# Transposes of a feed-forward's first chunk, and the affine step of two norms, placed differently in a fused three-block kernel

## The chip, the cores and the metric

The kernel runs on one core of a Trainium2 chip. The metric is the device time of one execution in microseconds (us); lower is better. The core has five engines with a queue of instructions each, and each works its queue in order: TensorE (PE, the matrix products), VectorE (DVE), ScalarE (ACT), GpSimd (POOL) and SyncE (SP, which here only starts DMAs).

## What is computed

The input x has 256 tokens of 1024 features, all in float32. A first block runs once: modulation of x by a vector c, an attention and convolution mixer, a layer norm, a gated feed-forward, a second layer norm. Two more layers follow: gated linear attention, feed-forward and a gate; then differential attention, feed-forward and a gate. Of the reference, what the change touches:

```python
def layer_norm(x, g, b):
    mu = mean(x); var = mean(square(x - mu))
    return (x - mu) * rsqrt(var + EPS) * g + b

# first block
x = layer_norm(ALPHA * x + g1 * mix, ln1_g, ln1_b)                 # norm 1
ff = swiglu(modulate(x, sh2, sc2), w_gate, w_up, w_down)           # feed-forward 0
x = layer_norm(ALPHA * x + g2 * ff, ln2_g, ln2_b)                  # norm 2

def swiglu(h, w_gate, w_up, w_down):                               # D_FF = 2816
    return (silu(h @ w_gate) * (h @ w_up)) @ w_down

# end of each of the two layers
h = h + swiglu_2(rms_norm(h), w_in, w_out)                         # feed-forwards 1 and 2
h = h + sigmoid(rms_norm(h) @ ple_w_gate) * (p @ ple_w_proj)
```

## The kernel before

**Products.** The tokens are two tiles of 128 (`t` = 0, 1). Every float32 product is made of three faster ones: an operand is split into a rounded part and a remainder (`xh`, `xl` for activations, `wh`, `wl` for weights), and `mm3` issues `xh*wh` (L159), `xh*wl` (L160) and `xl*wh` (L162). Weights come in granules of 128x1024: SP starts the DMA into `st`, ACT rounds it to `wh` (L150), DVE subtracts to get `wl` (L151). There are 11 buffers for `st` and 5 each for `wh` and `wl`. PSUM has four buffers of 128x512 for products (`mmb`) and four that hold sums for longer (`acb`).

**Order.** The code is a list of steps. A scheduler places each step in the queue of its engine when the program is built, by a cost model of its own, and puts in the waits. It may place a step earlier than the code does, where its operands allow, so what stands in a queue is not the order of the code alone.

**Activations for a product.** A tile of x is transposed by PE in blocks of 128x128 (`blocks_t`, L124) into an `acb`. `put` (L174) then makes `xh` on ACT (L177) and `xl` on DVE (L178). The two norms go through `put_affine` (L193): four ACT instructions per half of a tile (L197, one per block, 128x128) scale and shift the transposed block into `hT`, an SBUF tile with two buffers, and `put` works from there. The halves are `n` = 0 and 1.

**A norm** (`norm_tile`, L773, once for each `t`): DVE adds the product of the feed-forward or the mixer to x; ACT squares with a running sum (L785, `jk`); a few operations on one column give mean and inverse deviation (`mu`, one of them a power on POOL, L787); ACT normalizes each half of x in place (L791), PE transposes it, and `put_affine` follows with weight and offset folded into per-row scale and shift. The residual stream itself needs x times weight plus offset as well: `normed` (L798) multiplies by `g` (L799) and adds `b` (L800), each 128x1024 from a broadcast of the vector over all partitions (`bcast`, a DMA). Norm 1 has it on DVE, given as a fill to chunks 1 and 3 of the feed-forward behind it; norm 2 has it on POOL (`later`). `g2_part` and `g2_row` (L728 to L736) make a vector needed for norm 2 from a product with a column, between the two tiles of norm 1.

**A feed-forward** (`ffn`, L803): 11 chunks of 256 hidden columns. A chunk is four granules of 12 products each, 48 in all, into two `mmb`, one per tile, gate in the left half and up in the right half. The hidden part follows: silu on ACT (L833 in feed-forward 0, L836 in 1 and 2), times up on DVE (L834, L837) into `sg`, four transposes on PE (L124) into a third `mmb`, rounding on ACT (`hh`, L842) and remainder on DVE (`hl`). The second product of chunk c-1 stands between the first product of chunk c and its hidden part. Chunk 0 has nothing of that kind.

**The end** (`fin`, L901): per tile and half, sigmoid on ACT (L904), times a product on DVE (L905), added to x (L906), and a DMA to the output (L1139), 128x512 each.

Of the kernel before, what the change touches and what calls it, by code (L numbers as in the profile page):

```python
# [10 lines left out]
F32 = mybir.dt.float32  # L11
# [3 lines left out]
OP = mybir.AluOpType  # L15
# [67 lines left out]
def body(ctx, tc, d, out, dbg=None):  # L83
# [80 lines left out]
    class XT:  # L164
# [28 lines left out]
        def put_affine(self, t, n, ps, scale, shift, pool, **kw):  # L193
            m = pool.tile([P, 512], F32, name="hT", **kw)
            for i in range(4):
                j = slice(4 * n + i, 4 * n + i + 1)
                A.activation(m[:, i * P:(i + 1) * P], ps[:, i * P:(i + 1) * P], AF.Identity,  # L197
                             bias=shift[:, j], scale=scale[:, j])
            self.put(t, n, m)
# [89 lines left out]
    def block1(adp):  # L289
        with ExitStack() as es:  # L290
# [433 lines left out]
            out_rows(7)  # L724
            l1g = bcast(d["ln1_g"][0], D)
            l1b = bcast(d["ln1_b"][0], D)

            def g2_part(hf):  # L728
# [23 lines left out]
            g2_row(1, *g2[1])  # L752
        with tc.tile_pool(name="f1", bufs=1) as wk:
            acc = ffn(gate_up([(d["w_gate"][0], 0), (d["w_up"][0], 0)]), d["w_down"][0], hx, None, wk,
                      {1: lambda: normed(V, l1g, l1b, 0), 3: lambda: normed(V, l1g, l1b, 1)})
            hx = XT()
# [9 lines left out]
            def later(junk):  # L766
                for t in range(2):
                    normed(G, l2g, l2b, t)
                for t in range(2):
                    rms_of(t, junk, rs[t])  # L770
# [32 lines left out]
    def ffn(gu, wd, xt, rs, wk, fill={}, apart=False):  # L803
# [7 lines left out]

        for c in range(NCH):
            ps = [mm(), mm()]
            for g in range(KB // 2):
                wh, wl = gran(stage(gu(g, c)), (2, 512))
                for t in range(2):
                    for i in range(2):
                        kb = g * 2 + i
                        xh, xl = xt(kb, t)
                        mm3([ps[t]], xh, xl, [wh[:, i]], [wl[:, i]], kb == 0, kb == KB - 1)  # L820
            if c in fill:
                fill[c]()
            if 0 < c < NCH - 1:
                for i in range(2):
                    wh, wl = row_gran(wd, (c - 1) * 2 + i)
                    for t in range(2):
                        both(acc[t], *hid(c - 1, i)(t), wh, wl, c == 1 and i == 0, False)
            tp = mm()
# [14 lines left out]
            V.tensor_sub(hl, tv, hh.bitcast(F32))  # L843
            pend.append((hh, hl))
        late = []
        for c in range(NCH - 2, NCH):
# [50 lines left out]
    def ple_gate(i, xt, rs, pp, wk):  # L897
        acc = accs()
        kproj(d["ple_w_gate_2"][i], INORDER, xt, acc, 4, pool=wk, own=4)

        def fin(t, n):  # L901
            hs = slice(n * 512, n * 512 + 512)
            sg = wk.tile([P, 512], F32, name="sgm", tag="sgm", bufs=2)
            A.activation(sg, acc[t][n], AF.Sigmoid, scale=rs[t])  # L904
            V.tensor_mul(sg, sg, pp[t][:, hs])  # L905
            V.tensor_add(x[t][:, hs], x[t][:, hs], sg)  # L906
        return fin
# [200 lines left out]
    def tail_layer(i, acc, pp, nxt):  # L1108
        with tc.tile_pool(name=f"tl{i}", bufs=1) as wk:
# [25 lines left out]
            for t in range(2):  # L1135
                for n in range(2):
                    hs = slice(n * 512, n * 512 + 512)
                    fin(t, n)
                    Y.dma_start(out[0, t * P:(t + 1) * P, hs], x[t][:, hs])  # L1139

# [195 lines left out]
```

## Time and profile before

| | |
|---|---|
| median of 3 runs | 1066.44 us (1065.1 to 1066.7) |
| profiled execution | 1059.51 us |
| its span, from the first instruction to the last | 1057.7 us |
| granted TensorE clock, mean over the span | 0.991 of full speed |
| PE busy | 1014.9 us, 96% of the span |
| DVE busy | 631.4 us, 60% |
| ACT busy | 560.5 us, 53% |
| POOL busy | 56.3 us, 5% |
| DMA | 57% of the span of 16 engines, 183 GB/s from and to memory |

How to read it: an instruction waits in its queue until its operands are there, and all behind it on that engine wait too. The view of the timeline lists start, duration and, in brackets, the idle time just before and what ended it. The end of a product on PE is modelled, so that its duration overlaps the next one's start; the distance of starts is the time that it takes in a row of products. The chain of waits is followed back from the last instruction to whatever released each step. The rows are shown further down.

### The profile page before, as it was taken

The numbers are of one execution on the slowest core, as the hardware profiler recorded it, in microseconds if no ns is written. First come the engines' busy times: TensorE is split into PE (matmuls) and PEld (weight loads), VectorE is DVE, ScalarE is ACT, GpSimd is POOL, SyncE is SP. The second block draws the span as 40 slices with busy tenths as digits, with TensorE's granted clock in tenths as the row PEclk, the third lists the DMA queues.
The fourth block names the chain that finished last, engine by engine and source line by source line (L and its number), as shares of the span: only waits on it lengthen the run. The fifth ranks groups of instructions, "written<-read, shape, count | busy, mean of one in ns | idle before, by whom it ended". The sixth has DMA issues, their size and how long they took to land.

```text
span 1057.7 us, 13558 instructions
## 1 busy us (share of the span) xinstructions
PE 1014.9 (96%) x4883; PEld 810.6 (77%) x4883; DVE 631.4 (60%) x1021; ACT 560.5 (53%) x910; POOL 56.3 (5%) x47
## 2 busy tenths in 40 slices
PE   6899998999999999999999999999998999999998
PEld 3676675888888778887788888887777778888886
DVE  2378468555556466567554547578786655555654
ACT  2355448444454568465544446566857554444643
POOL 0000100000000130000000000004020100000000
PEclk9999999999999999999999999999999999999999
DMA  9958577866666155255666657535433365666601
GB/s 301 386 200 308 202 276 263 273 195 185 193 196 198 50 175 186 81 166 156 194 190 180 192 187 266 147 127 171 135 120 111 124 187 191 186 190 187 239 1 40
DMA packets 131640, 194.48 MB, mean 184 GB/s; under 512 B 10562, under 2 KB 93390, under 8 KB 131572
## 3 DMA queue, kind: packets, MB, share of 16 engines
q1 hardware_dynamic: 130792, 193.21, 57.0%
q8 instruction: 38, 0.62, 0.2%
q10 hardware_dynamic: 780, 0.40, 0.1%
q14 instruction: 30, 0.25, 0.1%
HBM read 192.53 MB, written 1.05 MB: 183 GB/s over the span
## 4 chain that ended last, share of the span: by engine, by line
PE 79%; DVE 8%; ACT 6%; DMA 2%; issue 2%; POOL 1%; SPq 0%; ACTq 0%; DVEq 0%; POOLq 0%
PE mmb L162 16%; PE mmb L159 16%; PE mmb L160 16%; PE acb L162 7%; PE acb L159 7%; PE acb L160 7%; DVE wl L151 2%; PE mmb L124 2%; ACT wh L150 1%; PE acb L124 1%; POOL rs L272 1%; ACT e L1202 1%; DMA st<-in_w_ada_dram 1%; PE mmb L333 1%; PE acb L333 1%
## 5 line engine op out<-in xcount | busy, mean ns | idle before, releaser
L151 DVE TENSOR_TENSOR wl<-st,wh 128x1024 fp32r<-128x1024 f32 (+4 forms) x292 | 350.9, 1207 | 240.1 <-ACT wh L150 237.2
L150 ACT CAST wh<-st 128x1024 fp32r<-128x1024 f32 (+4 forms) x292 | 300.6, 1038 | 280.6 <-PE mmb L162 143.6
L159 PE MATMUL mmb<-wh,xh 128*128 128x512 f32 (+4 forms) x888 | 353.4, 399 | 6.3 <-ACT xh L386 4.5
L160 PE MATMUL mmb<-wl,xh 128*128 128x512 f32 (+4 forms) x888 | 346.8, 391 | 2.1 <-DVE wl L151 2.1
L162 PE MATMUL mmb<-wh,xl 128*128 128x512 f32 (+4 forms) x888 | 342.8, 391 | 6.0 <-DVE xl L178 4.7
L159 PEld LDWEIGHTS mmb<-wh,xh 128*128 128x128 f32 x888 | 169.1, 191 | 44.7 <-ACT xh L386 6.3
L162 PEld LDWEIGHTS mmb<-wh,xl 128*128 128x128 f32 x888 | 169.1, 190 | 44.5 <-DVE xl L178 6.3
L160 PEld LDWEIGHTS mmb<-wl,xh 128*128 128x128 f32 x888 | 169.3, 191 | 33.3 <-DVE wl L151 2.8
L159 PE MATMUL acb<-wh,hh 128*128 128x512 f32 x216 | 84.0, 389 | 0.0
L160 PE MATMUL acb<-wl,hh 128*128 128x512 f32 x216 | 84.0, 389 | 0.0
L162 PE MATMUL acb<-wh,hl 128*128 128x512 f32 x216 | 66.6, 389 | 0.0
L159 PEld LDWEIGHTS acb<-wh,hh 128*128 128x128 f32 x216 | 40.6, 188 | 8.4
L162 PEld LDWEIGHTS acb<-wh,hl 128*128 128x128 f32 x216 | 40.5, 188 | 8.4
L160 PEld LDWEIGHTS acb<-wl,hh 128*128 128x128 f32 x216 | 40.5, 188 | 8.4
L866 POOL TENSOR_TENSOR rsx<-rsx,mhalf 128x1 f32<-128x1 f32 x12 | 10.2, 851 | 468.2 <-DVE rsx L865 468.2
L272 POOL TENSOR_TENSOR rs<-rs,mhalf 128x8 f32<-128x8 f32 (+1 forms) x14 | 20.0, 1433 | 241.1 <-DVE rs L271 241.1
L836 ACT ACTIVATE sg<-mmb,rsx 128x256 f32<-128x256 f32 x44 | 20.7, 474 | 22.2 <-PE mmb L162 20.4
L151 DVE TENSOR_TENSOR wxl<-st,wxh 128x1024 fp32r<-128x1024 f32 x22 | 26.7, 1219 | 3.1 <-ACT wxh L150 3.1
L837 DVE SCALAR_TENSOR_TENSOR sg<-mmb,rsx,sg 128x256 f32<-128x256 f32 x44 | 20.8, 480 | 11.1 <-ACT sg L836 11.1
L150 ACT CAST wxh<-st 128x1024 fp32r<-128x1024 f32 x22 | 22.7, 1052 | 5.1 <-PE acb L162 3.0
L124 PE MATMUL mmb<-ident,sg 128*128 128x128 f32 x132 | 21.1, 275 | 2.7 <-DVE sg L837 2.1
L843 DVE TENSOR_TENSOR hl<-mmb,hh 128x512 fp32r<-128x512 f32 x33 | 22.6, 685 | 1.8 <-ACT hh L842 1.8
(311 smaller groups left out, 1062.7 us busy)
## 6 DMA issues: line engine op xcount, KB each, us to landing
st<-in_ffn_w_in_dram SPq DMA_DIRECT2D x176, 256.0 KB
st<-in_ffn_w_out_dram SPq DMA_DIRECT2D x44, 512.0 KB
st<-in_w_ada_dram SPq DMA_DIRECT2D x32, 512.0 KB
st<-in_diff_w_in_dram SPq DMA_DIRECT2D x24, 512.0 KB
st<-in_w_gate_dram SPq DMA_DIRECT2D x44, 256.0 KB
st<-in_w_up_dram SPq DMA_DIRECT2D x44, 256.0 KB
st<-in_w_down_dram SPq DMA_DIRECT2D x22, 512.0 KB
st<-in_w_ada_dram SPq DMA_DIRECT2D x32, 256.0 KB
```

The source lines that it names most:

```text
L124: T.transpose(o, i, ident)
L150: A.copy(h[:, :n], src)
L151: V.tensor_sub(l[:, :n], src, h[:, :n].bitcast(F32))
L159: T.matmul(p_, xh, wh, start=start, stop=False)
L160: T.matmul(p_, xh, wl, start=False, stop=False)
L162: T.matmul(p_, xl, wh, start=False, stop=stop)
L272: G.tensor_tensor(r[:, :n], r[:, :n], mhalf[:, :n], op=OP.pow)
L333: T.matmul(bk[32 * j:32 * j + 32, :n], cB[:, kb, :], sts[kb // k][:, kb % k * n:kb % k * n + n], start=kb < 4, stop=kb >= 4)
L836: A.activation(sg, ps[t][:, 0:256], AF.Silu, scale=rs[t])
L837: V.scalar_tensor_tensor(sg, ps[t][:, 256:512], rs[t], sg, op0=OP.mult, op1=OP.mult)
L843: V.tensor_sub(hl, tv, hh.bitcast(F32))
L1202: A.activation(es_[:, i, :], b[:, i * S:(i + 1) * S], AF.Exp, bias=mx[:, i:i + 1], scale=rh[:, i:i + 1], accum_out=L[t][:, s, 2 * hp + i:2 ...
```

## The change

1. `put_affine`: the half n = 1 is scaled and shifted on DVE (four `tensor_scalar` from PSUM) and the half n = 0 stays on ACT.
2. Norm 1: the broadcasts of weight and offset are asked for in the fill of chunk 1 of feed-forward 0 and no longer in the mixer; `normed` for the tiles is the fill of chunks 3 and 5 rather than 1 and 3.
3. Norm 2: `normed` runs on DVE and no longer on POOL.
4. `ffn`: the hidden part is a function, `hidden`. That of chunk 0 is issued behind the first granule of chunk 1. All three feed-forwards use it.
5. The end: the last of the four pieces of the output is done in two halves of 256 columns, with a DMA each.

```diff
 def put_affine(self, t, n, ps, scale, shift, pool, **kw):
...
-                A.activation(m[:, i * P:(i + 1) * P], ps[:, i * P:(i + 1) * P], AF.Identity,
-                             bias=shift[:, j], scale=scale[:, j])
+                if n:
+                    V.tensor_scalar(m[:, i * P:(i + 1) * P], ps[:, i * P:(i + 1) * P], scale[:, j], shift[:, j],
+                                    op0=OP.mult, op1=OP.add)
+                else:
+                    A.activation(m[:, i * P:(i + 1) * P], ps[:, i * P:(i + 1) * P], AF.Identity,
+                                 bias=shift[:, j], scale=scale[:, j])
...
-            l1g = bcast(d["ln1_g"][0], D)
-            l1b = bcast(d["ln1_b"][0], D)
...
+            ln1 = []
             acc = ffn(gate_up([(d["w_gate"][0], 0), (d["w_up"][0], 0)]), d["w_down"][0], hx, None, wk,
-                      {1: lambda: normed(V, l1g, l1b, 0), 3: lambda: normed(V, l1g, l1b, 1)})
+                      {1: lambda: ln1.extend((bcast(d["ln1_g"][0], D), bcast(d["ln1_b"][0], D))),
+                       3: lambda: normed(V, *ln1, 0), 5: lambda: normed(V, *ln1, 1)})
...
-                    normed(G, l2g, l2b, t)
+                    normed(V, l2g, l2b, t)
...
+        first = None
+        for c in range(NCH):
+            ps = [mm(), mm()]
+            for g in range(KB // 2):
...
+                if c == 1 and g == 0:
+                    hidden(first)
...
+            if c == 0:
+                first = ps
+            else:
+                hidden(ps)
...
-                    fin(t, n)
-                    Y.dma_start(out[0, t * P:(t + 1) * P, hs], x[t][:, hs])
+                    for h in range(2) if t and n else (None,):
+                        hs = slice(n * 512, n * 512 + 512) if h is None else slice(512 + h * 256, 768 + h * 256)
+                        fin(t, n, h)
+                        Y.dma_start(out[0, t * P:(t + 1) * P, hs], x[t][:, hs])
```

What it does to the queues follows. Operands have the numbers that the program gives them (`wh_4405` is one granule), and the line numbers of the changed kernel are a few higher: there L198 is the new affine step on DVE, L201 the one on ACT, L802 and L803 are `normed`, L788 is `jk`, L794 the normalizing and L821 the silu of feed-forward 0.

PE, feed-forward 1, from the end of chunk 0 (products with `wh_4384`) into chunk 1; before:

```order
L159 MATMUL mmb_4323<-wh_4384,xh_4298 128x512
L160 MATMUL mmb_4323<-wl_4385,xh_4298 128x512
L162 MATMUL mmb_4323<-wh_4384,xl_4299 128x512
L124 MATMUL mmb_4400<-ident_82,sg_4401 128x128 x2
L159 MATMUL mmb_4415<-wh_4420,xh_4250 128x512
L124 MATMUL mmb_4400<-ident_82,sg_4406 128x128 x2
L160 MATMUL mmb_4415<-wl_4421,xh_4250 128x512
L162 MATMUL mmb_4415<-wh_4420,xl_4251 128x512
```

And now:

```order
L159 MATMUL mmb_4323<-wh_4384,xh_4298 128x512
L160 MATMUL mmb_4323<-wl_4385,xh_4298 128x512
L162 MATMUL mmb_4323<-wh_4384,xl_4299 128x512
L160 MATMUL mmb_4400<-wl_4406,xh_4250 128x512
L162 MATMUL mmb_4400<-wh_4405,xl_4251 128x512
...
L159 MATMUL mmb_4401<-wh_4405,xh_4282 128x512
L160 MATMUL mmb_4401<-wl_4406,xh_4282 128x512
L162 MATMUL mmb_4401<-wh_4405,xl_4283 128x512
L124 MATMUL mmb_4421<-ident_82,sg_4422 128x128 x2
L124 MATMUL mmb_4421<-ident_82,sg_4427 128x128 x2
L159 MATMUL mmb_4400<-wh_4439,xh_4250 128x512
```

The transposes of `sg` stood right behind the last product of chunk 0, and stand 12 products later, behind the first granule of chunk 1 (`wh_4405`). The same holds in feed-forwards 0 and 2.

DVE, norm 2, from the first remainder of tile 0 (`xl_3181`; `xl_3196` is its second half, `xl_3226` and `xl_3241` are tile 1); before:

```order
L178 TENSOR_TENSOR xl_3181<-hT_3175,xh_3180 128x512
L178 TENSOR_TENSOR xl_3196<-hT_3190,xh_3195 128x512
L178 TENSOR_TENSOR xl_3226<-hT_3220,xh_3225 128x512
L151 TENSOR_TENSOR wl_3341<-st_3337,wh_3340 128x832
L151 TENSOR_TENSOR wl_3411<-st_3408,wh_3410 128x768
L178 TENSOR_TENSOR xl_3241<-hT_3235,xh_3240 128x512
L151 TENSOR_TENSOR wl_3429<-st_3426,wh_3428 128x768
L151 TENSOR_TENSOR wl_3447<-st_3444,wh_3446 128x768
```

And now:

```order
L198 TENSOR_SCALAR hT_3190<-acb_3185,gb2_3151 128x128 x4
L178 TENSOR_TENSOR xl_3181<-hT_3175,xh_3180 128x512
L802 TENSOR_TENSOR x0_87<-x0_87,bc_3083 128x1024
L178 TENSOR_TENSOR xl_3196<-hT_3190,xh_3195 128x512
L803 TENSOR_TENSOR x0_87<-x0_87,bc_3085 128x1024
L198 TENSOR_SCALAR hT_3235<-acb_3230,gb2_3151 128x128
L178 TENSOR_TENSOR xl_3226<-hT_3220,xh_3225 128x512
L198 TENSOR_SCALAR hT_3235<-acb_3230,gb2_3151 128x128 x3
L151 TENSOR_TENSOR wl_3341<-st_3337,wh_3340 128x832
L802 TENSOR_TENSOR x1_88<-x1_88,bc_3083 128x1024
L178 TENSOR_TENSOR xl_3241<-hT_3235,xh_3240 128x512
L803 TENSOR_TENSOR x1_88<-x1_88,bc_3085 128x1024
```

Eight affine steps and the four instructions of `normed`, on x0 and x1, have come in between the remainders, and POOL has lost its four.

DVE, norm 1, around the remainders of tile 0 (`xl_1564` before, `xl_1560` now; `part` belongs to `g2_part`); before:

```order
L731 TENSOR_TENSOR part_1535<-acb_1526,bias2_126 128x512
L783 TENSOR_SCALAR mu_1612<-bst_1605 128x1
L151 TENSOR_TENSOR wl_1685<-st_1681,wh_1684 128x1024
L784 TENSOR_SCALAR mu_1612<-mu_1612 128x1
L799 TENSOR_TENSOR x0_87<-x0_87,bc_1436 128x1024
L178 TENSOR_TENSOR xl_1564<-hT_1558,xh_1563 128x512
L731 TENSOR_TENSOR part_1600<-acb_1591,bias2_126 128x512
L800 TENSOR_TENSOR x0_87<-x0_87,bc_1438 128x1024
L178 TENSOR_TENSOR xl_1579<-hT_1573,xh_1578 128x512
L786 TENSOR_SCALAR mu_1612<-bst_1605 128x1
L788 TENSOR_TENSOR mu_1612<-mu_1612 128x1
```

And now:

```order
L732 TENSOR_TENSOR part_1531<-acb_1522,bias2_126 128x512
L198 TENSOR_SCALAR hT_1569<-acb_1564,m2_136 128x128 x4
L732 TENSOR_TENSOR part_1596<-acb_1587,bias2_126 128x512
L786 TENSOR_SCALAR mu_1608<-bst_1601 128x1
L151 TENSOR_TENSOR wl_1681<-st_1677,wh_1680 128x1024
L178 TENSOR_TENSOR xl_1560<-hT_1554,xh_1559 128x512
L178 TENSOR_TENSOR xl_1575<-hT_1569,xh_1574 128x512
L787 TENSOR_SCALAR mu_1608<-mu_1608 128x1
L151 TENSOR_TENSOR wl_1700<-st_1696,wh_1699 128x1024
L151 TENSOR_TENSOR wl_1719<-st_1715,wh_1718 128x1024
L789 TENSOR_SCALAR mu_1608<-bst_1601 128x1
```

The multiplication and addition on x0 have gone behind both remainders of tile 0 and behind three more weight remainders, though still ahead of the remainders of tile 1; four affine steps and a `part` are ahead of `xl_1560`.

ACT, norm 1, from the rounding of tile 0 to the normalizing of tile 1 (`x1`); before:

```order
L177 CAST xh_1563<-hT_1558 128x512
L197 ACTIVATE hT_1573<-acb_1568,m2_136 128x128 x3
L736 COPY g2row_61<-acb_1526 128x512
L177 CAST xh_1578<-hT_1573 128x512
L785 ACTIVATE jk_1604,bst_1605<-x1_88,mu_1612 128x1024
L736 COPY g2row_61<-acb_1591 128x512
L150 CAST wh_1703<-st_1700 128x1024
L791 ACTIVATE x1_88<-x1_88,mu_1612 128x512 x2
```

And now:

```order
L150 CAST wh_1699<-st_1696 128x1024
L177 CAST xh_1559<-hT_1554 128x512
L177 CAST xh_1574<-hT_1569 128x512
L737 COPY g2row_61<-acb_1522 128x512
L737 COPY g2row_61<-acb_1587 128x512
L150 CAST wh_1718<-st_1715 128x1024
L150 CAST wh_1739<-st_1736 128x1024
L788 ACTIVATE jk_1600,bst_1601<-x1_88,mu_1608 128x1024
```

Four affine steps are gone, and two more granules (`wh_1718`, `wh_1739`) are rounded ahead of the squares of x1 (`jk`). On PE all 24 products of tile 0 in chunk 0 now stand ahead of the eight transposes of x1, where the first four stood behind 13 of them before.

## Rows read from the trace of the kernel before

**Rows 1.** The page, busy time of each engine, its share of the span, instructions.

```profile
PE 1014.9 (96%) x4883; PEld 810.6 (77%) x4883; DVE 631.4 (60%) x1021; ACT 560.5 (53%) x910; POOL 56.3 (5%) x47
```

**Rows 2.** The chain of waits, chunk 0's end in feed-forward 1: start us, us, what.

```profile
504.99 1.28 ACT L836
506.28 0.48 ACT sg L836
506.79 0.50 DVE sg L837
...
508.69 0.23 PE mmb L159
```

**Rows 3.** Timeline of PE there: start, us, instruction, idle time before and its releaser.

```profile
505.88 0.39 PE L162 MATMUL mmb<-wh,xl 128*128 128x512 f32 x1
507.33 0.44 PE L124 MATMUL mmb<-ident,sg 128*128 128x128 f32 x2 [1.07 <-DVE sg L837]
```

**Rows 4.** Timeline of PE, the same place in feed-forward 2.

```profile
852.83 0.39 PE L162 MATMUL mmb<-wh,xl 128*128 128x512 f32 x1
854.28 0.44 PE L124 MATMUL mmb<-ident,sg 128*128 128x128 f32 x2 [1.07 <-DVE sg L837]
```

**Rows 5.** Timeline of PE, the same place in feed-forward 0.

```profile
183.08 0.39 PE L162 MATMUL mmb<-wh,xl 128*128 128x512 f32 x1
184.06 0.44 PE L124 MATMUL mmb<-ident,sg 128*128 128x128 f32 x2 [0.58 <-DVE sg L834]
```

**Rows 6.** Timeline of POOL in norm 2.

```profile
366.54 2.35 POOL L799 TENSOR_TENSOR x<-x,bc 128x1024 f32<-128x1024 f32 x1 [3.18 <-ACT pp L892]
...
377.36 2.97 POOL L800 TENSOR_TENSOR x<-x,bc 128x1024 f32<-128x1024 f32 x1
```

**Rows 7.** Timeline of DVE in norm 2.

```profile
367.50 1.94 DVE L178 TENSOR_TENSOR xl<-hT,xh 128x512 fp32r<-128x512 f32 x1 [3.60 <-ACT xh L177]
...
370.53 1.69 DVE L178 TENSOR_TENSOR xl<-hT,xh 128x512 fp32r<-128x512 f32 x1 [1.09 <-ACT xh L177]
372.80 0.69 DVE L178 TENSOR_TENSOR xl<-hT,xh 128x512 fp32r<-128x512 f32 x1 [0.58 <-ACT xh L177]
...
378.03 2.86 DVE L178 TENSOR_TENSOR xl<-hT,xh 128x512 fp32r<-128x512 f32 x1
```

**Rows 8.** Timeline of PE in norm 2.

```profile
369.50 0.71 PE L162 MATMUL mmb<-wh,xl 128*128 128x416 f32 x1 [1.33 <-DVE xl L178]
...
380.94 0.46 PE L162 MATMUL mmb<-wh,xl 128*128 128x416 f32 x1 [1.90 <-DVE xl L178]
```

**Rows 9.** The chain of waits in norm 2, products of 416 columns.

```profile
371.25 0.35 PE mmb L159
...
373.17 0.19 PE mmb L159
```

**Rows 10.** Stretches of norm 2: busy us (instructions) by engine, granted clock, DMA share, GB/s.

```profile
370.00:373.00 3.00, 3.00 (x10) 2.85 (x9) 1.89 (x2) 3.00 (x7) 1.67 (x1) 0.53 0.02 5
...
sum 23.00, PE 19.09 PEld 17.07 DVE 12.70 ACT 17.67 POOL 12.04; mean PE 3.18 PEld 2.85 DVE 2.12 ACT 2.95 POOL 2.01
```

**Rows 11.** What PE waits for from 158 to 188: us in total, times, longest.

```profile
PE mmb L162 <- DVE xl L178: 1.5, 2, 0.9
PE mmb L159 <- ACT xh L177: 0.7, 1, 0.7
```

**Rows 12.** Groups by shape: line, engine, operation xcount | busy, mean ns | idle before.

```profile
L191 DVE SCALAR_TENSOR_TENSOR xl<-acb,cols,xh 128x128 fp32r<-128x128 f32 x56 | 16.8, 345 | 0.8 <-ACT xh L190 0.6
...
L799 DVE TENSOR_TENSOR x<-x,bc 128x1024 f32<-128x1024 f32 x2 | 2.4, 1221 | 1.1 <-PE acb L124 1.1
```

**Rows 13.** Timeline of ACT in norm 1.

```profile
168.08 1.19 ACT L785 ACTIVATE jk<-x,mu 128x1024 f32<-128x1024 f32 x1
...
170.28 1.05 ACT L150 CAST wh<-st 128x1024 fp32r<-128x1024 f32 x1
```

**Rows 14.** The chain of waits in norm 1, a product of `g2_row`.

```profile
168.90 0.87 PE acb L735 x2
```

More of the change, by code (lines that the diff above doesn't have):

```diff
@@ L810, in hid, with hidden @@
             return lambda t: (hh[:, i, t * P:(t + 1) * P], hl[:, i, t * P:(t + 1) * P])
[L812 to L827, printed above, removed]
+        def hidden(ps):
             tp = mm()
@@ L844, in ffn @@
             pend.append((hh, hl))
+        first = None
+        for c in range(NCH):
+            ps = [mm(), mm()]
+            for g in range(KB // 2):
+                wh, wl = gran(stage(gu(g, c)), (2, 512))
+                for t in range(2):
+                    for i in range(2):
+                        kb = g * 2 + i
+                        xh, xl = xt(kb, t)
+                        mm3([ps[t]], xh, xl, [wh[:, i]], [wl[:, i]], kb == 0, kb == KB - 1)
+                if c == 1 and g == 0:
+                    hidden(first)
+            if c in fill:
+                fill[c]()
+            if 0 < c < NCH - 1:
+                for i in range(2):
+                    wh, wl = row_gran(wd, (c - 1) * 2 + i)
+                    for t in range(2):
+                        both(acc[t], *hid(c - 1, i)(t), wh, wl, c == 1 and i == 0, False)
+            if c == 0:
+                first = ps
+            else:
+                hidden(ps)
         late = []
@@ L899, in ple_gate, with fin @@
         kproj(d["ple_w_gate_2"][i], INORDER, xt, acc, 4, pool=wk, own=4)
[L901 to L904, printed above, removed]
+        def fin(t, n, h=None):
+            ps, o, w = (acc[t][n], n * 512, 512) if h is None else \
+                (acc[t][n][:, h * 256:h * 256 + 256], n * 512 + h * 256, 256)
+            hs = slice(o, o + w)
+            sg = wk.tile([P, 512], F32, name="sgm", tag="sgm", bufs=2)[:, 0:w]
+            A.activation(sg, ps, AF.Sigmoid, scale=rs[t])
             V.tensor_mul(sg, sg, pp[t][:, hs])
@@ L1136, in tail_layer @@
                 for n in range(2):
-                    hs = slice(n * 512, n * 512 + 512)
-                    fin(t, n)
-                    Y.dma_start(out[0, t * P:(t + 1) * P, hs], x[t][:, hs])
+                    for h in range(2) if t and n else (None,):
+                        hs = slice(n * 512, n * 512 + 512) if h is None else slice(512 + h * 256, 768 + h * 256)
+                        fin(t, n, h)
+                        Y.dma_start(out[0, t * P:(t + 1) * P, hs], x[t][:, hs])
     hx, rs = tail_layer(0, acc, pp, True)
```

## Prediction, made before the changed kernel was run

> **What bounds the kernel now.** I read the page first, for who is busy: PE for 1014.9 of 1057.7 us, DVE and ACT for little over half [rows 1]. So the kernel can lose only what PE idles or runs slow, some 43 us in all, and an edit is worth what it takes from PE's waits at its place. Then I read the chain of waits at each place that the change touches, and the timeline of PE, DVE and POOL there. Three kinds of loss stand at these places.
>
> At the end of chunk 0 of a feed-forward PE has nothing left but the transposes, which wait for silu and multiplication: in feed-forward 1 the chain goes through 1.28 us in which ACT does something at the silu's line that isn't the silu, 0.48 of silu and 0.50 of multiplication [rows 2]. The products are 0.23 us apart [rows 2], so the last one, begun at 505.88, gave PE back at 506.11, and the transposes begin at 507.33: 1.22 us lost [rows 3]. Feed-forward 2 loses the same, 854.28 less 853.06 [rows 4], feed-forward 0 0.75 us, 184.06 less 183.31 [rows 5].
>
> In norm 2 two remainders `xl` take 1.94 and 2.86 us on DVE, where one of the same shape takes 0.69 [rows 7]. Beside the long ones POOL is in `normed` [rows 6]; at the short one it is idle. Both long ones end 0.55 to 0.56 us behind POOL's instruction (366.54 + 2.35 = 368.89 against 369.44; 380.33 against 380.89), which is what a subtraction does that can get on only when POOL has finished. PE waits 1.33 and 1.90 us for them [rows 8]. Behind the first wait the granted clock is 0.53 for 3 us [rows 10], which is the lower level of 1.2 GHz for nearly all of them, and products of 416 columns are 0.35 us apart rather than 0.19 [rows 9]; nine of them lose 9 x 0.16 = 1.4 us. So norm 2 loses 1.3 + 1.9 + 1.4 = 4.6 us to these two.
>
> In norm 1 PE waits 1.5 us for remainders and 0.7 for a rounding [rows 11]; the multiplication and addition of `normed`, 1.22 us each on DVE [rows 12], stand among them.
>
> **The change, part by part.** The sum is made against the profiled execution's 1059.51 us. The median of the runs, 1066.44, is 1.0065 times that; a saving is scaled so at the end.
>
> *First chunk's transposes.* The four move behind 12 products of chunk 1, 12 x 0.23 = 2.7 us of work that PE has in any case. The chain that they wait for is 1.28 + 0.48 + 0.50 = 2.26 us; it began at 504.99, when tile 0 of the chunk was complete, 1.1 us ahead of PE's last product. So 1.1 + 2.7 = 3.8 us cover 2.3, and the second tile's silu and multiplication, another 0.5 to 1.0, still fit. In feed-forward 0 the roundings of two more granules come between the two silus on ACT, 1.05 us each [rows 13]. There the tiles go one after the other, so tile 0's silu has 5 us and more of cover, and both roundings wait only for buffers that PE leaves before tile 1 is complete; then tile 1's silu and multiplication, 0.9 us, have nine products, 2.0 us, ahead of its transposes. I cost the wait that is left at nothing, and up to 0.4 us in each feed-forward if the cover fails. What is next late is the second product of chunk 0, and it has another 36 products ahead of it. Saved: 1.22 + 1.22 + 0.75 = 3.2 us, bounds 2.0 and 3.7; the upper one since two or three products of chunk 1 go into short waits at the chunk's start.
>
> *Norm 2, `normed` to DVE.* POOL's four instructions go, and four of 1.22 us come to DVE [rows 12]. DVE is busy 12.7 of 23 us in this stage [rows 10], of which 1.25 + 2.17 for the two long remainders, and 1.0 in a third, are lengthening; 8.3 are work. With 4 x 1.22 and the eight affine steps it has some 15.6 us of work in a stage of 19. The row nearest to an affine step on DVE is the operation from PSUM on 128 columns with a scalar, 345 ns [rows 12]; a quarter of the 0.69 us for 512 columns [rows 7], 0.17, is the lower bound. I take 0.3, as it is close to the first: 1.2 us a half. Placed on the times of the trace, `xl` of tile 0's first half runs 367.5 to 368.2, the affine half before it being ready while DVE was idle (3.60 us idle ahead of it [rows 7]). The second half's goes behind the multiplication on x0, 369.4 to 370.0, where it ended at 372.2 [rows 7]. The last, for which PE waited at 380.94, ends near 376; PE gets there near 376 too, as it hasn't lost 1.3 and 1.4 us before. The change adds a wait on ACT: the last rounding of `xh` now stands behind one more granule's rounding, which waits for PE to release a buffer; behind it are the last `xl` on DVE, the addition on x1, and PE. I price that at 0.4. Saved: 4.6 - 0.4 = 4.2 us. Bounds: 2.4 if the clock falls all the same and 0.4 more is waited; 4.6 if nothing is waited for in their place.
>
> What the lengthening is, decides whether it goes. The Trainium skill, "SBUF — State Buffer", section "Who interferes with whom", says that a VectorE instruction with two SBUF inputs and a GpSimd instruction that reads SBUF exclude each other for a whole instruction, and that the loser blocks fully rather than sharing. The remainder from `hT` is of that form, and the 0.55 us behind POOL's end in the rows above agree. By that page all 3.4 us of lengthening vanish with POOL's work; if DVE were slow for another reason, memory traffic say, the sum would be the 3.2 us of the first step alone.
>
> *Norm 1.* On DVE, ahead of the first remainder, 1.22 us of multiplication go, and four affine steps (1.2) and an addition of 512 columns (0.69, as the subtraction [rows 7]) come: 0.7 later, so that PE's wait there, 1.5 - 0.9 = 0.6 [rows 11], becomes 1.3. One product of `g2_row`, 0.87 us [rows 14], goes out of tile 0's row on PE into this wait. On ACT, ahead of the squares of x1, which began at 168.08, two roundings of 1.05 come [rows 13] and four affine steps go; on DVE a weight remainder of 1.2 is now ahead of x1's scale. Of these 3.3 us the affine steps give back some 1.0 (by the 0.3 that I take for one), so x1 is normalized 2.3 us later. PE has in that time all 24 products of tile 0, 5.5 us, and by the times of the trace it then waits some 0.75 us for x1's transposes and, as before, some 1.6 (0.7 and 0.9 [rows 11]) between these and tile 1's products. In all 1.3 + 0.75 + 1.6 less 0.87 is 2.8, against 2.2 of before: 0.6 lost. Bounds: 2.2 saved, if all waits of [rows 11] go, and 2.9 lost, if x1's 2.3 us come on the path whole beside the 0.6. The moved broadcasts cost nothing: SP starts each stage when a buffer is free, the two come two stages later in its queue than before, and the multiplications that need them come behind the norm; without that cover they are two transfers of 512 KB, as much as two granules.
>
> *The end.* Three operations on 512 columns follow the last product, some 0.69 us each as a subtraction of that size [rows 7], 2.1 in all; on 256 columns one is 0.48 to 0.50 [rows 2], and by halves the chain is one on ACT and four on DVE, 2.4 in all, with half the bytes in the last transfer. I take 0, bounds -0.3 and +0.4.
>
> Sum: 3.2 + 4.2 - 0.6 + 0 = 6.8 us: 1052.7 in the profiled execution, 1059.6 for the median.
>
> **Rivals.**
> *A. The clock takes some back.* Any wait over a microsecond that is left in norm 2 or comes in norm 1 may be followed by the low clock, as that of 1.33 us was [rows 8, 9]: 1.4 us each. For it: norm 1 comes to a wait of 1.3 us by my own placing. Against it: behind the 1.2 us of a first chunk the products are 0.23 us apart as ever [rows 2]. One such fall: 5.4 us saved, 1061.0. The Trainium skill, "TensorE: Matmul & The Clock Gate", section "HAM oscillation — how this bites in real kernels", has idle gaps between groups of matmuls bring the slow state back; the row of 0.53 agrees, that behind the first chunk doesn't.
> *B. The change doesn't do in the norms what it says*: the lengthening had another cause, or DVE's own added work takes its place. Only the feed-forwards gain: 3.2 us, 1063.2. Against it: the short remainder with POOL idle.
> *C. Slower: DVE becomes the bound in both norms.* It gets 4.9 us of `normed` and 2.4 of affine steps in norm 2, 2.4 in norm 1, and PE works in order behind its remainders. If all 9.7 us come on the path, less 3.4 of lengthening and 3.2 of the feed-forwards, it is 3.1 us slower, 1069.6. It decides from where DVE has no idle time left in norm 2, that is from 11 us of added work or if affine steps take over 0.7 us; 15.6 of 19 speak against it.
> *D. More is saved*: x1 is no later in norm 1, which then saves 1.5 rather than losing 0.6, and products that fill short waits at the chunks' starts give 0.9: 9.8 us, 1056.6.
>
> **How the numbers follow.** The measurement can tell 0.2%, 2.1 us, from no change. Chances: forecast 0.45, A 0.20, B 0.14, C 0.11, D 0.10. Faster: 0.45 + 0.10 + 0.18 of A + 0.08 of B = 0.81. The same: 0.02 of A, 0.06 of B, 0.02 of C = 0.10. Slower: 0.09 of C. The range goes from 1054, D with 2.6 us of what the upper bounds leave, to 1064.5, B with 1.2 us of uncovered transposes; it leaves out C and a few hundredths at either end.
>
> **What would show it.** In the trace after: transposes of the first chunks without idle time before them, and the chain through products there (first step). In norm 2 remainders of 0.69 us, no wait of PE over half a microsecond and a granted clock near 1.0 from 370 to 373. In norm 1 one longer wait ahead of x1's tile, and a stage that is longer by no more than a microsecond. The forecast is wrong if remainders in norm 2 stay long with POOL idle, if an affine step on DVE takes over 0.5 us, or if x1's transposes come more than 4 us later than before.

## The result, and the profile after

The changed kernel takes 1056.61 us (median of 5 runs, 1055.67 to 1060.54), the kernel before 1066.34 beside it (5 runs, 1061.7 to 1066.7). The ratio is 0.9925, 95% interval 0.9908 to 0.9943: 8.0 us saved, between 6.1 and 9.8. 1059.6 was predicted, with a range of 1054.0 to 1064.5: 6.8 us saved by the sum. Measured again beside other runs of before, the ratio was 0.9928 (0.9908 to 0.9948).

The two profiled executions are only 3.8 us apart, 1059.51 and 1055.70. That of before was a short one, 7 us under its median, and most of this lies where nothing was changed: the first transposes of norm 1 begin at 162.86 us in it, and in the thirteen other profiles of this study between 161.5 and 171.0, 167.3 in the middle, whatever the kernel. So stages are compared here and not whole executions. The head of the page after:

```profile
span 1053.9 us, 13554 instructions
...
PE 1015.8 (96%) x4883; PEld 811.2 (77%) x4883; DVE 636.7 (60%) x1043; ACT 554.8 (53%) x895; POOL 49.5 (5%) x43
```

**Feed-forwards.** Timeline of PE in feed-forward 1, where the rows of before are [rows 3]:

```profile
508.06 0.39 PE L160 MATMUL mmb<-wl,xh 128*128 128x512 f32 x1
508.28 0.39 PE L162 MATMUL mmb<-wh,xl 128*128 128x512 f32 x1
508.51 0.60 PE L124 MATMUL mmb<-ident,sg 128*128 128x128 f32 x4
508.87 0.48 PE L159 MATMUL mmb<-wh,xh 128*128 128x512 f32 x1
```

The four transposes stand together, 12 products later, with no idle time before them. In [rows 3] they waited 1.07 us. A product near the start of the chunk comes sooner too, 0.39 us behind the one before it (which begins at 496.08) rather than 0.66 (496.14); the first row is of before, the second of after:

```profile
496.80 0.50 PE L159 MATMUL mmb<-wh,xh 128*128 128x512 f32 x1 [0.16 <-ACT xh L190]
```

```profile
496.47 0.73 PE L159 MATMUL mmb<-wh,xh 128*128 128x512 f32 x2
```

**Norm 2.** Timeline of DVE, against [rows 7]; L198 is the affine step on DVE, L802 the multiplication that POOL had:

```profile
368.68 1.36 DVE L198 TENSOR_SCALAR hT<-acb,gb 128x128 f32<-128x128 f32 x4 [2.55 <-PE acb L124]
369.96 0.68 DVE L178 TENSOR_TENSOR xl<-hT,xh 128x512 fp32r<-128x512 f32 x1
370.56 1.21 DVE L802 TENSOR_TENSOR x<-x,bc 128x1024 f32<-128x1024 f32 x1
371.70 0.68 DVE L178 TENSOR_TENSOR xl<-hT,xh 128x512 fp32r<-128x512 f32 x1
...
373.76 0.68 DVE L178 TENSOR_TENSOR xl<-hT,xh 128x512 fp32r<-128x512 f32 x1
...
377.38 0.68 DVE L178 TENSOR_TENSOR xl<-hT,xh 128x512 fp32r<-128x512 f32 x1
```

All four remainders (L178) take 0.68 us, where three took 1.69 to 2.86. What PE waits for from 361 to 386 us, and the stretch of [rows 10] where the clock was 0.53 (busy us of PE, PEld, DVE, ACT, POOL, then granted clock, DMA share, GB/s):

```profile
PE mmb L159 <- ACT xh L177: 0.7, 1, 0.7
PE mmb L159 <- ACT ph L892: 0.5, 1, 0.5
```

```profile
370.00:373.00 3.00, 2.93 (x17) 2.56 (x17) 3.00 (x5) 3.00 (x8) 0.00 (x0) 1.00 0.03 5
```

The waits of 1.33 and 1.90 us [rows 8] and the low clock behind the first are gone. What is left is 0.7 us for the first rounding and 0.5 in another branch, both there before too; the prediction had named as a sign that no wait over half a microsecond would be left, and these two are over it.

**Norm 1.** What PE waits for from 158 to 192 us, against [rows 11], and DVE ahead of the first remainders:

```profile
PE mmb L159 <- ACT xh L177: 1.5, 1, 1.5
PE acb L124 <- ACT x L794: 0.6, 1, 0.6
PE mmb L162 <- DVE xl L178: 0.3, 1, 0.3
```

```profile
167.96 1.36 DVE L198 TENSOR_SCALAR hT<-acb,m 128x128 f32<-128x128 f32 x4
...
169.96 1.22 DVE L151 TENSOR_TENSOR wl<-st,wh 128x1024 fp32r<-128x1024 f32 x1
171.09 1.29 DVE L178 TENSOR_TENSOR xl<-hT,xh 128x512 fp32r<-128x512 f32 x2
```

The waits have moved, 0.3, 0.6 and 1.5 us, and their sum, 2.4, is what it was (2.2 in [rows 11] and 0.2 more for x1, which has no row there).

**Stage by stage.** Each number is the distance of two starts in PE's timeline: from the first transposes of norm 1 to those of chunk 1 in feed-forward 0; from the first transposes of norm 2 to its last product of 416 columns; from there to the transposes that open feed-forward 1; and from the transposes that open feed-forwards 1 and 2 to those of their chunk 1. A star stands for each fall of the granted clock that begins in the stage; what one costs stands in the section on the clock.

| us | norm 1, start of ff 0 | norm 2 | linear attention | start of ff 1 | start of ff 2 |
|---|---|---|---|---|---|
| before | 38.06 | 23.89 * | 109.05 * | 32.38 | 32.33 |
| after | 37.06 | 18.97 | 111.68 * * | 30.86 | 30.80 |
| after, second trace | 37.18 | 18.95 | 110.01 * | 30.84 | 30.81 |
| after, third trace | 38.49 * | 18.98 | 109.73 * | 30.83 | 30.79 |
| first chunk alone | 37.32 | 23.81 * | 108.97 | 30.84 | 30.81 |
| norm 2 off POOL alone | 38.11 | 21.33 * | 108.58 | 32.38 | 32.33 |
| affine steps alone | 37.31 | 25.56 * | 110.26 | 32.38 | 32.35 |
| broadcasts alone | 38.05 | 23.90 * | 109.53 * | 32.39 | 32.35 |
| all but the affine steps | 37.31 | 20.24 | 110.51 * | 30.86 | 30.81 |
| all, norm 2 still on POOL | 37.08 | 25.79 * | 110.17 | 30.86 | 30.81 |
| before, POOL in 8 pieces | 38.04 | 20.34 | 109.86 * | 32.39 | 32.32 |

Where the clock doesn't fall, a stage whose queues are the same repeats to 0.15 us, the linear attention excepted. The stages hold the same products in all these kernels, but for the border of norm 2. One product of 384 columns that stood ahead of it before stands behind it in the changed kernel; three do in norm 2 off POOL alone, affine steps alone, all but the affine steps and all with norm 2 on POOL. They are 0.17 us each, so 4.7 of the 4.9 us by which norm 2 is shorter are a gain. Norm 2 and linear attention together take 132.9, 132.8 and 133.4 us in the three kernels that have before's queues there (before, first chunk alone, broadcasts alone), 133.05 in the mean, and 130.65, 128.96 and 128.71 in the three traces of the changed one, 129.44. So of norm 2's 4.9 us, 3.6 are left at the end of the linear attention.

### The profile page after: what moved, and what is told of

It is laid out like the page before. It is cut to its first block, busy times and chain, and to the rows that moved or that the text cites. A ratio compares the mean times of both kernels' runs of the same rounds, so it can differ in the third digit from the quotient of the medians.

```text
span 1053.9 us, 13554 instructions
## 1 busy us (share of the span) xinstructions
PE 1015.8 (96%) x4883; PEld 811.2 (77%) x4883; DVE 636.7 (60%) x1043; ACT 554.8 (53%) x895; POOL 49.5 (5%) x43
## 4 chain that ended last, share of the span: by engine, by line
PE 82%; DVE 7%; ACT 4%; DMA 3%; issue 2%; POOL 1%; SPq 0%; ACTq 0%; DVEq 0%; POOLq 0%
PE mmb L162 17%; PE mmb L159 17%; PE mmb L160 17%; PE acb L162 7%; PE acb L159 7%; PE acb L160 7%; DVE wl L151 2%; PE mmb L124 2%; PE acb L124 1%; POOL rs L276 1%; PE acb L337 1%; ACT wh L150 1%; DMA st<-in_w_ada_dram 1%; ACT e L1217 1%; PE mmb L337 1%
## 5 line engine op out<-in xcount | busy, mean ns | idle before, releaser
L874 ACT ACTIVATE junk<-x 128x1024 f32<-128x1024 f32 x10 | 10.6, 1059 | 25.3 <-DVE x L867 23.8
```

## Experiments: one part at a time

**First chunk alone.** The kernel before with the change in `ffn`:

```diff
+                if c == 1 and g == 0:
+                    hidden(first)
...
+            if c == 0:
+                first = ps
+            else:
+                hidden(ps)
```

> Of the change, only the first chunk's hidden part behind the first granule of chunk 1, in all three feed-forwards; queues elsewhere as before. The prediction's step: no idle time of PE before the first transposes of sg (0.58, 1.07 and 1.07 us before), 3.2 us saved, ratio 0.997. By the trace of the changed kernel, where the stretch from the transposes of x to the second chunk's transposes of sg is 1.5 us shorter in feed-forwards 1 and 2: 3.8 us or more, ratio 0.9964. If the gap only moves (to the second product of chunk 0): no change, 1.000.

Measured: ratio 0.9964 (0.9942 to 0.9987), 3.8 us. The stages say the same: 0.74 in feed-forward 0, 1.54 and 1.52 in 1 and 2, together 3.8. What PE waits for in feed-forward 1 there, from 490 to 515 us:

```profile
PE mmb L162 <- DVE xl L191: 0.2, 1, 0.2
```

No wait for `sg` is left, and nothing is late behind it: the gap didn't move on to the second product of chunk 0.

**Norm 2 off POOL alone.**

```diff
-                    normed(G, l2g, l2b, t)
+                    normed(V, l2g, l2b, t)
```

> Of the change, only the multiplication and addition of norm 2 on DVE rather than on POOL; affine steps stay on ACT. Theory of the lock: remainders xl of 128x512 in norm 2 take 0.69 us each, where three took 1.7 to 2.9; but with the affine steps on ACT the multiplications stand ahead of the remainders in DVE's queue, so PE still waits, some 0.7 to 1.5 us; 2 to 4 us saved, ratio 0.996 to 0.998. Rival (DVE slow for another reason, or its own added 4.9 us in place of the lock): xl still over 1 us, or waits of PE of over 3 us in norm 2, no change or slower.

Measured: 0.9957 (0.9937 to 0.9977), 4.6 us. DVE and PE in norm 2:

```profile
370.93 1.23 DVE L799 TENSOR_TENSOR x<-x,bc 128x1024 f32<-128x1024 f32 x1 [2.55 <-PE acb L124]
372.19 1.22 DVE L800 TENSOR_TENSOR x<-x,bc 128x1024 f32<-128x1024 f32 x1
373.33 0.68 DVE L178 TENSOR_TENSOR xl<-hT,xh 128x512 fp32r<-128x512 f32 x1
```

```profile
374.07 0.72 PE L162 MATMUL mmb<-wh,xl 128*128 128x416 f32 x1 [1.41 <-DVE xl L178]
```

The remainder takes 0.68 us at once, but it stands behind both instructions on x0, and PE waits 1.41 for it. The stage is 2.6 us shorter, 2.0 for the same products, and with the linear attention it is 3.1 (129.9 against 133.05); the rest of the 4.6 lies within the interval.

**Affine steps alone.**

```diff
+                if n:
+                    V.tensor_scalar(m[:, i * P:(i + 1) * P], ps[:, i * P:(i + 1) * P], scale[:, j], shift[:, j],
+                                    op0=OP.mult, op1=OP.add)
```

> Of the change, only the second half's affine step on DVE, in both norms; POOL keeps norm 2's multiplication and addition. The prediction's step for norm 1: 0.6 us lost there. By the trace of the changed kernel norm 1 with the gap of feed-forward 0 gains 1.0, so norm 1 alone 0 to 0.3 us gained. In norm 2 the theory of the lock has remainders of 1.7 us and more beside POOL as before, while affine steps, which read PSUM and no second SBUF operand, stay near 0.35; so norm 2 changes by less than 1 us. In all within 1 us of before, ratio 0.999 to 1.001. If the affine steps were what saves norm 2: 3 us or more, 0.997.

Measured: 1.0016 (0.9992 to 1.0040), no change that can be told, rather slower. POOL and DVE in norm 2:

```profile
370.64 2.37 POOL L803 TENSOR_TENSOR x<-x,bc 128x1024 f32<-128x1024 f32 x1 [3.18 <-ACT pp L896]
373.09 2.73 POOL L804 TENSOR_TENSOR x<-x,bc 128x1024 f32<-128x1024 f32 x1
375.77 2.84 POOL L803 TENSOR_TENSOR x<-x,bc 128x1024 f32<-128x1024 f32 x1
```

```profile
371.82 4.54 DVE L178 TENSOR_TENSOR xl<-hT,xh 128x512 fp32r<-128x512 f32 x2
```

With the affine steps out of ACT's way POOL starts its second pair sooner and works without a break, and two remainders together take 4.54 us. Norm 2 gets 1.7 us longer, where less than 1 was expected: PE's waits in it come to 5.7 us rather than 4.4. A fall of the clock is in it as it was before. In norm 1 the stage is 0.75 us shorter, and by its waits this is the gap at the first chunk of feed-forward 0: with all of tile 0's products ahead of tile 1's, PE waits for no `sg` any more. The first chunk's new place closes the same gap, so the two gains don't add up (37.06 to 37.18 with both, 37.32 with one).

**Broadcasts alone.**

```diff
-            l1g = bcast(d["ln1_g"][0], D)
-            l1b = bcast(d["ln1_b"][0], D)
...
+                      {1: lambda: ln1.extend((bcast(d["ln1_g"][0], D), bcast(d["ln1_b"][0], D))),
```

> Of the change, only the place of norm 1's broadcasts and fills. No engine's queue differs but SP's. The prediction costs it at nothing: ratio 1.000. In the trace of the changed kernel PE came to norm 1 3.2 us later than before, of which 1.6 us behind a low clock near 142 us. If the moved transfers do that, this kernel is 1 to 3 us slower, 1.001 to 1.003, and comes to norm 1 that much later; if it differs from one execution to the next, it is as before within 1.5 us there.

Measured: 0.9995 (0.9974 to 1.0016). No stage changes. Norm 1 begins at 165.74 us, in the midst of the other profiles.

**All but the affine steps**, and **the changed kernel again**:

> The change without its affine steps on DVE (all eight of each norm on ACT). The prediction gives the affine steps a loss of 0.6 us in norm 1 and all of norm 2's gain to POOL's work, so this would be as fast as the full change or a little faster, 0.992. By the traces of the single parts: norm 1 loses the 0.75 us that the affine steps gained there; norm 2, to the last product of 416 columns, takes 21.3 us as with POOL's work moved alone, where the full change takes 19.0. If the parts need each other, 2 to 3 us slower than the full change, 0.994 to 0.995.

> The changed kernel again, beside the runs of this chip: ratio 0.990 to 0.995 if the first measurement holds. For its trace: if the low clock behind the wait of 2.45 us at 481 us (1.5 us lost, in the trace of after alone) belongs to the change, it is there again; if it differs from one execution to the next, it may be missing, and the stretch from the last product of 416 columns to the transposes of feed-forward 1 is 110 us rather than 111.7. Norm 1 with the start of feed-forward 0 stays at 37.1 us, feed-forward 1 and 2 at 30.8, norm 2 at 19.0 to the last product of 416 columns: these differ by less than 0.3 if they belong to the order of the queues.

Measured: 0.9924 (0.9899 to 0.9949) without them, 0.9928 (0.9908 to 0.9948) with them. Norm 2 is 1.3 us longer without, norm 1 0.2, and the whole is no slower: what the affine steps give is within what can be told. They matter the other way: with POOL still at work norm 2 is longer with them (25.6 and 25.8 us, 23.9 before).

**All, norm 2 still on POOL.** The changed kernel with `normed(G, l2g, l2b, t)`:

> The changed kernel with norm 2's multiplication and addition back on POOL, whole (128x1024). The prediction gives this part 4.2 us of the 6.8: ratio 0.9965. By the traces norm 2 to the last product of 416 columns takes 24 to 25.6 us rather than 19.0, so 5 us or more slower than the changed kernel, 0.997 to 0.998; remainders beside POOL's instructions take 1.7 us or more.

Measured: 0.9989 (0.9968 to 1.0010). Of 0.72 to 0.75% only 0.11 are left, so the move off POOL is worth some 6.5 us in the company of the affine steps, and 4.6 alone, each uncertain by 2 to 3 us. The stages give 6.5 and 3.1 for norm 2 and the linear attention together. Norm 2 takes 25.79 us, with the remainders in pairs again:

```profile
367.20 4.54 DVE L178 TENSOR_TENSOR xl<-hT,xh 128x512 fp32r<-128x512 f32 x2
...
374.80 3.44 DVE L178 TENSOR_TENSOR xl<-hT,xh 128x512 fp32r<-128x512 f32 x2
```

## Experiments: POOL against DVE

**POOL in pieces.** The kernel before, with norm 2's work still on POOL, but cut:

```diff
-        eng.tensor_mul(x[t], x[t], g)
-        eng.tensor_add(x[t], x[t], b)
+        for q in range(8 if eng is G else 1):
+            w = D // 8 if eng is G else D
+            s = slice(q * w, q * w + w)
+            eng.tensor_mul(x[t][:, s], x[t][:, s], g[:, s])
+            eng.tensor_add(x[t][:, s], x[t][:, s], b[:, s])
```

> The kernel before, with norm 2's multiplication and addition still on POOL but in eight pieces of 128 columns each. Theory of the lock (one instruction of POOL excludes the remainder for its whole length): a remainder waits for one short piece at most, or for a piece between its own, so xl takes 0.7 to 1.2 us instead of 1.7 to 2.9, and PE's waits of 1.33 and 1.90 us shrink below 0.9 each. Rival (both share a rate, or DVE is slowed by something else): xl still takes 1.7 us or more while POOL works, as POOL's work is no less.

One execution, 1055.08 us; POOL and DVE in norm 2:

```profile
366.31 0.87 POOL L803 TENSOR_TENSOR x<-x,bc 128x128 f32<-128x128 f32 x2
...
368.42 0.88 POOL L803 TENSOR_TENSOR x<-x,bc 128x128 f32<-128x128 f32 x2
...
374.30 2.03 POOL L803 TENSOR_TENSOR x<-x,bc 128x128 f32<-128x128 f32 x2
```

```profile
366.70 1.02 DVE L178 TENSOR_TENSOR xl<-hT,xh 128x512 fp32r<-128x512 f32 x1 [3.60 <-ACT xh L177]
368.97 0.87 DVE L178 TENSOR_TENSOR xl<-hT,xh 128x512 fp32r<-128x512 f32 x1 [1.25 <-ACT xh L177]
371.24 0.73 DVE L178 TENSOR_TENSOR xl<-hT,xh 128x512 fp32r<-128x512 f32 x1 [1.40 <-ACT xh L177]
...
375.07 0.94 DVE L178 TENSOR_TENSOR xl<-hT,xh 128x512 fp32r<-128x512 f32 x1
```

The remainders take 0.73 to 1.02 us, though POOL works beside all of them. So what stretched them was not POOL's work but the length of one instruction of it: the remainder waits for a piece of some 0.4 us, not for one of 2.4 to 3.0. PE's waits for remainders are 0.38 us and less, the clock doesn't fall in norm 2, and it takes 20.34 us, about as with the work on DVE and the affine steps on ACT (20.24, with three products fewer). POOL pays as well: two pieces take 2.03 us, with DVE in remainders all the while, where two others take 0.87.

The Trainium skill, "SBUF — State Buffer", section "Who interferes with whom", has the two exclude each other for a whole instruction; these rows agree, with 0.73 to 1.02 us behind short instructions against 1.69 to 2.86 behind long ones [rows 7].

**POOL in pieces for both norms**, on the changed kernel: `normed(G, ...)` for norm 1 too, in eight pieces.

> The changed kernel with the multiplications and additions of both norms on POOL in eight pieces of 128 columns. Theory: what costs time is the length of POOL's single instruction, not that POOL works; so remainders of 0.7 to 1.2 us, no wait over 0.9 us in norm 2, and DVE free of 9.8 us of work in the two norms. Norm 1 with the start of feed-forward 0 as in the changed kernel, 37.1 us or up to 0.5 less; norm 2 to the last product of 416 columns 19.0 to 20.0. Ratio 0.991 to 0.993, no slower than the changed kernel. Rival: POOL's pieces collide with the weight remainders on DVE all along, and the kernel is over 2 us slower than the changed one, 0.995.

Measured: 0.998 (0.9959 to 1.0001): 5.5 us slower than the changed kernel. Norm 2 is as good (19.18 us), but norm 1 with the start of feed-forward 0 takes 42.06 us. POOL, DVE and PE there:

```profile
177.51 1.85 POOL L804 TENSOR_TENSOR x<-x,bc 128x128 f32<-128x128 f32 x2
179.33 0.86 POOL L805 TENSOR_TENSOR x<-x,bc 128x128 f32<-128x128 f32 x2
180.16 0.55 POOL L790 TENSOR_TENSOR mu<-mu,mhalf 128x1 f32<-128x1 f32 x1
```

```profile
177.16 0.14 DVE L789 TENSOR_SCALAR mu<-bst 128x1 f32<-128x1 f32 x1
...
180.74 0.16 DVE L791 TENSOR_TENSOR mu<-mu 128x1 f32<-128x1 f32 x1 [2.10 <-POOL mu L790]
```

```profile
181.86 1.56 PE L124 MATMUL acb<-ident,x 128*128 128x128 f32 x8 [2.96 <-ACT x L794]
```

The power for x1's deviation (L790) is an instruction of POOL. It stands behind the pieces of x0, is done at 180.71, and x1's scale, its transposes and PE follow 2 to 3 us late. The pieces that DVE slowed (1.85 us for two) make it later still. That is some half of the 5 us: PE's waits in the stage come to 5.0 us rather than 2.4. The other half goes with the clock, which falls behind the wait of 2.96 us; it is 0.51 in the mean from 182.8 to 189.8 us, of which:

```profile
185.00:190.00 5.00, 5.00 (x13) 3.89 (x14) 2.38 (x4) 3.19 (x4) 4.85 (x10) 0.53 0.69 270
```

Neither of the two expectations saw this: what was queued on POOL behind the moved work.

**Affine steps block by block**, odd blocks on DVE; first on the changed kernel, then with POOL's pieces:

```diff
-                if n:
+                if i % 2:
                     V.tensor_scalar(
```

> The changed kernel, with the affine steps shared by ACT and DVE block by block (odd blocks on DVE) rather than by half tile. If what is left of PE's waits, 1.54 us in norm 1 and 0.69 in norm 2 for the rounding of the first half, is the row of four steps on ACT, each shrinks by 0.7 and the kernel is about 1 us faster than the full change, 0.9915. Rival: the order that the scheduler makes of it puts multiplications of 1.2 us ahead of the steps on DVE, and the waits grow by 1 us or more: 0.993 or above.

> As the run before, and the affine steps shared block by block. With no multiplications in DVE's way, the wait of 1.54 us in norm 1 and of 0.69 in norm 2 for the first half's rounding shrink by some 0.7 each, and it is 1 to 1.5 us faster than the changed kernel: ratio 0.9905 to 0.992. Rival: the waits belong to something other than the row of four steps on ACT (the roundings of granules ahead of it), and nothing is gained: 0.9925.

Measured: 0.9979 (0.9962 to 0.9996) and 0.9976 (0.9953 to 0.9998), both slower than the changed kernel. In the first, the scheduler puts the multiplication on x1 between the steps of its own halves, as the rival had it; ACT's rounding and then PE wait for the steps:

```profile
183.69 0.95 DVE L198 TENSOR_SCALAR hT<-acb,m 128x128 f32<-128x128 f32 x2
184.56 1.22 DVE L802 TENSOR_TENSOR x<-x,bc 128x1024 f32<-128x1024 f32 x1
185.69 0.72 DVE L198 TENSOR_SCALAR hT<-acb,m 128x128 f32<-128x128 f32 x2
```

```profile
186.80 0.79 PE L159 MATMUL mmb<-wh,xh 128*128 128x512 f32 x1 [2.87 <-ACT xh L177]
```

PE waits 2.87 us where it waited 1.54, with a fall of the clock at its end, and norm 1 with the start of feed-forward 0 takes 39.68 us. Norm 2 takes 21.86, with waits of 1.30 and 0.76 us for remainders. In the second, norm 1 has the same late power and the same low clock as the run before (42.41 us). The runs show no version to be faster than the changed kernel.

## Experiments: the clock

In the trace of the changed kernel the clock falls no more in norm 2, but does behind PE's wait at the end of the linear attention, which was 1.82 us long before and without a fall. PE's timeline and the stretch around it, after:

```profile
481.36 0.50 PE L160 MATMUL mmb<-wl,xh 128*128 128x512 f32 x1 [2.45 <-DVE wl L151]
```

```profile
481.00:486.00 5.00, 4.64 (x14) 3.72 (x15) 2.24 (x5) 0.00 (x0) 0.00 (x0) 0.69 0.60 189
```

And of the kernel before with POOL in pieces:

```profile
479.01 0.50 PE L160 MATMUL mmb<-wl,xh 128*128 128x512 f32 x1 [2.36 <-DVE wl L151]
```

```profile
481.00:483.00 2.00, 2.00 (x11) 1.65 (x10) 0.50 (x1) 0.00 (x0) 0.00 (x0) 1.00 0.87 273
```

A wait of 2.45 us, and 1.6 us lost behind it; a wait of 2.36, and nothing. What such a fall costs can be read here, since PE has the same products and no other wait from there to the transposes of feed-forward 1: 10.39 us with the fall, 8.74 without. In all fourteen traces it is 10.33 to 10.39 with one and 8.74 to 8.77 without. The second trace of the changed kernel had the fall as well, and so had the one without affine steps. A third trace was made for it:

> The changed kernel a third time, for its trace alone. In both traces of it so far, and in the one without the affine steps, the clock falls behind PE's wait of 2.1 to 2.5 us at the end of the linear attention (1.4 to 1.5 us lost), which it does in no trace of a kernel with another queue. If it belongs to this order of the queues it is there again, and the stretch from the last product of 416 columns to the transposes of feed-forward 1 is 110.0 us or more; if it comes by the execution, it may be missing, and the stretch is 108.6 us. The waits and the stages of the norms and the feed-forwards are as in the two traces before, within 0.15 us.

Measured, 1056.17 us: the fall is there, behind a wait of 1.88 us. So three traces of the changed kernel and that of all but the affine steps have it, and the ten other kernels' traces have none there, with waits of 1.3 to 2.4 us. The length of the stretch, 109.73 us, would have said otherwise by the expectation; it differs too much to serve for that. In the table every trace has one or two falls between the start of norm 2 and feed-forward 1; the two kernels with POOL's pieces in both norms, which aren't in it, have none. The change took the one behind norm 2's wait away, and one came at the end of the linear attention. Four against ten suggest that it belongs to the order of the queues, but three of the four are one program, and no other kernel was traced twice, so that isn't shown. What in the order would bring it is open: the kernel with the steps block by block (above) has the same parts and no fall there.

The third trace also has a fall in norm 1, behind the wait of 1.5 us that the other two show without one:

```profile
181.54 0.50 PE L159 MATMUL mmb<-wh,xh 128*128 128x512 f32 x1 [1.53 <-ACT xh L177]
```

```profile
183.00:186.00 3.00, 3.00 (x9) 2.31 (x7) 2.08 (x3) 1.02 (x1) 0.00 (x0) 0.51 1.08 407
```

So 1.3 to 1.4 us of that stage come and go from one execution of a program to the next. The Trainium skill, "TensorE: Matmul & The Clock Gate", section "HAM oscillation — how this bites in real kernels", has idle gaps bring the slow state. In norm 1, norm 2 and at the end of the linear attention every fall here stands close behind a wait of 1.3 us or more or at its end, which agrees, though the gaps of the page's example are longer; but more than half of such waits have none behind them.

## Why the prediction was right, and where it was off

**First chunk: 3.2 predicted, 3.8 measured.** Feed-forward 0 gave the 0.75 that was read (0.74). Feed-forwards 1 and 2 gave 1.53 each rather than 1.22. The term was mis-sized by 0.3 in each: 0.27 us is the short wait at the chunk's start (0.39 rather than 0.66 us to the next product, above), and some 0.05 that the four transposes stand in one group rather than in two pairs. Products of chunk 1 in short waits were in the prediction's upper bound, not in its sum. That a product of chunk 1 fills this one is inferred from the queue: the first of its three products with `wh_4405` no longer stands with the other two.

**Norm 2: 4.2 predicted, 4.7 measured for the same products (4.9 in the stage).** All three terms went: the waits of 1.33 and 1.90 and the 1.4 of low clock make 4.6; the 0.4 that was put down for the rounding behind a granule did not come: PE has no wait in the second half of the stage. The mechanism held, by the row that the prediction named (0.68 us each), and by the pieces, which separate the length of the instruction from the work. The prediction didn't say what the affine steps give to it: without them norm 2 keeps one wait of 1.41 us, and the runs don't tell the kernel from the changed one. The affine step takes 0.40 us in the mean,

```profile
L198 DVE TENSOR_SCALAR hT<-acb,gb 128x128 f32<-128x128 f32 x8 | 2.8, 399 | 2.5 <-PE acb L124 2.5
```

where 0.3 was taken and 0.345 was the nearest row, though four in a row take 1.36; DVE had the time for it.

**Norm 1: 0.6 lost predicted, 0.2 gained measured.** The waits came as worked out, 0.27 after the first remainder (1.3 less a product of 0.87 was predicted, 0.43), 0.56 before x1's transposes (0.75) and 1.54 behind them (1.6): together 2.4. x1's transposes begin 11.6 us behind those of x0, 9.2 before, so 2.35 later, where 2.3 was worked out. The step that failed is the other side of the comparison: the waits of before were put at 2.2, from two rows, and left out 0.2 us for x1's normalizing; the three terms of after were 0.4 too high together; the last 0.2 was not traced. The sign was wrong, the size within the bounds.

**The end: 0 predicted, 0.25 gained**, from 29.07 to 28.82 us between the last transposes and the end, within the bounds. No run has it alone, but the eight traces with the two halves lie between 28.78 and 28.82, the six without between 29.07 and 29.09. **Broadcasts: nothing**, as predicted.

**Rival A happened in part, at a place that the prediction didn't look at.** The stages give 3.8 + 4.7 + 0.2 + 0.25 = 9.0 us; 1.1 of norm 2's gain are given back by the end of the linear attention, and 7.9 are left, which is what the runs say (7.7 and 8.0). In the 1.1 are a fall of the clock at the end, 1.6 us, and waits there that are 0.3 longer in the mean; some 0.9 less at the stage's start, where two of the three traces have no fall, go against them. The prediction looked for such a fall in the norms alone. Its own 6.8 came near since its three terms were too small together by 1.9, the end by 0.25, and this one was missing: that is luck in part. Rival B fell with the rows of 0.68 us. Rival C fell too, but its mechanism showed in the run with POOL's pieces in both norms and in that with steps block by block: there work put ahead of a late step did come on the path, in stages longer by 5 and 2.6 us, of which waits of PE are 2.6 and 1.7 and most of the rest goes with the low clock behind them. Rival D's 9.8 us is near what the stages give without what was given back, but not by its parts: norm 1 saved 0.2 and not 1.5.

## What to carry to other kernels

A short instruction on one engine that is stretched to end a fixed time behind a long one on another is waiting for that instruction, and in norm 2 cutting the long one into pieces helped as much as moving it: look at ends, not at durations. Before work is moved to an idle engine, look for the one-column instruction that the critical chain sends through that engine's queue. And where a first pass of a loop ends in a chain over three engines, let one block of the next pass stand in front of it; here that was half of the gain.

## What was not expected of the hardware

Remainders and POOL's pieces slow each other both ways: two pieces of 128 columns took 0.87 us, and 2.03 with DVE in remainders all the while. A VectorE step from PSUM on 128 columns took 0.40 us, longer than the operation of the same shape with one input more (0.345). And the low clock behind waits of one and the same length, 1.5 us in norm 1, came in one of three executions of one program.
